# Unused tiles of 64, 192 and 160 bytes ahead of three operand pools in a one-core transformer block

## The chip, the core and the metric

One core of a Trainium2 chip runs the whole kernel. The time is device microseconds from launch to end; the value is the median of several executions. One further execution is taken by the hardware profiler and gives the page and the trace. TensorE (PE in the profile) multiplies: it loads a 128x128 *stationary* operand from SBUF (the row PEld, an LDWEIGHTS instruction) and then streams a *moving* operand of up to 512 columns through it (the row PE, a MATMUL instruction); the product goes to PSUM. VectorE (DVE), ScalarE (ACT) and GpSimd (POOL) do the elementwise work, SyncE (SP) issues the DMAs.

## The reference

One layer of a diffusion backbone on 1024 latent tokens of 1024 channels, with 256 context tokens, in float32. Cut to what is computed:

```python
h  = modulate(rmsnorm(x, g_pre1), sh1, sc1)          # shifts, scales, gates: silu(c) @ w_mod
q, k, v, f, g_a, g_f = split_proj(h @ w_in)          # 1024 x 3328
attn = banded_window_attention(rope(q), rope(k), v, kc, vc, sink)
y  = (sigmoid(g_a) * (attn @ w_pa) + sigmoid(g_f) * (fourier_mix(f) @ w_pf)) @ w_out
x  = x + gt1 * rmsnorm(y, g_post1)
h2 = modulate(rmsnorm(x, g_pre2), sh2, sc2)
u, gate = split(h2 @ w_up)                           # 1024 x 5632
x  = x + gt2 * rmsnorm((silu(conv3(u)) * gate) @ w_down, g_post2)
```

## The kernel before

**Arithmetic.** Every float32 product is made of three passes: each operand is split into a rounded part `hi` (ScalarE) and the remainder `lo` (VectorE or GpSimd), and `mm3` (L83 to L87) issues hi·hi on L85, hi·lo on L86 and lo·hi on L87, each a MATMUL of 512 columns with a fresh 128x128 stationary operand. The three large products (with `w_in`, `w_up`, `w_down`) go by Winograd's form of Strassen's scheme: `wino` (L208) takes *pairs* of weight blocks, and for each pair seven products P1 to P7, so an *item* is one product of one pair, 3 MATMULs for each of its k-blocks (4 in `w_in` and `w_up`, 2 or 3 in `w_down`). Between products, ScalarE and VectorE take results out of PSUM and prepare the next stationary operands.

**Where the operands lie.** The stationary operands (names `hP`, `lP`, `bP`) are 2048-byte tiles of the pool `spool` (`s`, L60). The moving operands are sums of activations or, in the down projection, of `w_down` blocks, with names B11, B21, T1, T2, T3, T4n, B22 (`dB`, `dT` in the down projection). They lie in tiles of 6144 and 2048 bytes that `hb_tiles` (L164) takes from three pools:

- `hb1` (L448, right side of SBUF): all seven moving operands of the product with `w_in`. In the first 80 us some of its tiles also receive `w_mod` blocks.
- `hbl` (L1519, left side, after the small tiles of `small`): B11 and B21 of the product with `w_up`, that is P1 and P2; half of `w_out` (`w0a`, `w0b`); and in the down projection the slots 0 and 1, and half of slot 7, of the rotation in `d_place` (L1734).
- `hb2` (L1928, right side, allocated when the pool `ow` is released): the other five moving operands of `w_up` and the other slots of the down projection.

Pools on the left grow upward in the order of their allocation, pools on the right downward from the top. In the built program every tile of `spool` starts 224 bytes past a multiple of 256, and every tile of `hb1` and `hb2` as well; the tiles of `hbl` start 192 bytes past one. So moving minus stationary address, modulo 256, is 0 for `hb1` and `hb2` and 224 (32 bytes short) for `hbl`. In the attention, the moving operands `kst` and `kc` start at 224 and the stationary queries `qs` (pool `miscA`, left side) at 0.

**Order.** The stages follow each other: norm and modulation with the first items of `w_in` (to about 80 us), the rest of `w_in` (to 335), attention and Fourier mixing (to 530), `w_pa` and `w_out` (to about 690), `w_up` (to about 1120), `w_down` (to the end). Most of it is in blocks of `tc.manual_schedule()`, so engines run in the order of the code. Each engine runs its own queue in order. At the change's place between `ow.release()` (L1927) and `mm(0)` (L1938) the first `w_up` products begin.

Of the kernel before, what the change touches and what calls it, by code (L numbers as in the profile page):

```python
# [10 lines left out]
F = mybir.dt.float32  # L11
# [5 lines left out]
P = 128  # L17
# [18 lines left out]
def fbits(ap):  # L36
    return ap.bitcast(F)
# [3 lines left out]
def block_kernel(ctx: ExitStack, tc: tile.TileContext, t: dict, out: bass.AP, dbg: dict):  # L41
    nc = tc.nc
    PSUM = bass.MemoryType.PSUM

    def pool(name, bufs=1, side=None, space=None):
        kw = {}
        if side:
            kw["side"] = side
        if space:
            kw["space"] = space  # L50
        return tc.alloc_tile_pool(name=name, bufs=bufs, reuse_waits="tile", **kw) if space != bass.MemoryType.DRAM else tc.alloc_tile_pool(name=name, bufs=bufs, space=space)
# [8 lines left out]
    def s(name, dtype=F):  # L60
        return spool.tile([P, 512], dtype, tag="s", name=name, bufs=40)
# [14 lines left out]
    def mul(out, a, b, eng=None):  # L76
        return tt(out, a, b, ALU.mult, eng)

    def split(hi, lo, src, lo_eng=None):
        copy(hi, src)  # L80
        sub(lo, src, fbits(hi), lo_eng)
# [27 lines left out]


    small = pool("small", 1, side="left")

    def tiny(name, n, bufs=4, dtype=F):
        return small.tile([P, n], dtype, tag=f"ty{n}", name=name, bufs=bufs)
# [49 lines left out]
    def hb_tiles(hp, ops, n, ta="ha", tb="hb"):  # L164

        res = {}
        for o in ops:
            a = [hp.tile([P, 3, 512], R, tag=ta, name=f"{o}a{i}", bufs=n) for i in range(2)]
            b = [hp.tile([P, 1, 512], R, tag=tb, name=f"{o}b{i}", bufs=n) for i in range(2)]
            res[o] = list(zip(a, b))  # L170
        return res
# [262 lines left out]
    def ps(name):  # L434
        return psA.tile([P, 512], F, tag="ps", name=name, bufs=8)
# [9 lines left out]
    nc.scalar.activation(out=small.tile([P, 1], F, name="warm"), in_=sv[:, 0:1], func=AF.Sqrt, scale=0.0)  # L445
    mul(sv, sv, vec[:, VC:VC + 16])

    hbp = pool("hb1", 1, side="right")  # L448
    hb = hb_tiles(hbp, ("B11", "T1"), 4, "ga", "gb")

# [417 lines left out]
    def late_loads(i):  # L868
        if i == 0:
            c128.append(s("c128"))  # L870
            load(out=c128[0][:, :2 * P], in_=t["dftc"])
            alt.append(s("alt"))
            load(out=alt[0], in_=t["alt"].to_broadcast([P, 512]))
        elif i == 1:
            for j in range(4):
                wkv[j] = s(f"wkv{j}")
                load(out=wkv[j].rearrange("p (k c) -> p k c", k=2),
                     in_=w_in[j * 256:(j + 1) * 256, K0:K0 + 256].rearrange("(k p) c -> p k c", p=P))
        elif i == 2:
            for j in range(4):  # L880
                wr = wkv[j]
                wkv[j] = (s(f"wkvh{j}", R), s(f"wkvl{j}", R))
                split(*wkv[j], wr)
        elif i == 3:
            for h in range(2):
                vT.append(s(f"vT{h}"))
                load(out=vT[h], in_=v_d[:, h * 512:(h + 1) * 512])
        else:
            for j in range(2):
                dtr[0, j] = s(f"dt0{j}")  # L890
                load(out=dtr[0, j], in_=t["dft"][0, j * P:(j + 1) * P, :])
# [213 lines left out]
    with tc.manual_schedule():  # L1105
        lead(NI - 5)
        lead(NI - 4)
        mm(NI - 5)
        evac(NI - 5)
        for i in range(3, 5):  # L1110
            late_loads(i)
        mm(NI - 4)
        after(NI - 4)
        mm(NI - 3)
        evac(NI - 3)
        c128, alt = c128[0], alt[0]
        ptu = ps("ptu")
        nc.tensor.matmul(ptu[:, :8], c128[:, :P], tu[:, :8], start=True, stop=True)
        nc.tensor.matmul(ptu[:, 8:12], c128[:, P:2 * P], tu[:, 8:12], start=True, stop=True)
        mm(NI - 2)  # L1120
        mm(NI - 1)
        misc.release()
        hbp.release()


        mid = pool("mid", 1, side="right")
        miscA = pool("miscA", 1, side="left")

        def m2(name, dtype=F):
            return mid.tile([P, 512], dtype, tag="m", name=name, bufs=28)  # L1130

        def mp(name, w, dtype=F):
            return mid.tile([P, 640], dtype, tag="p", name=name, bufs=12)[:, :w]

        def m4(name, dtype=F):
            return mid.tile([P, 1024], dtype, tag="l", name=name, bufs=6)

        dtab = {}

        def dft_table(w):  # L1140
            for j in range(2):
                if w == 0:
                    hi, lo = m2(f"dth{w}{j}", R), m2(f"dtl{w}{j}", R)
                else:
                    hi, lo = mp(f"dth{w}{j}", 512, R), mp(f"dtl{w}{j}", 512, R)
                split(hi, lo, dtr[w, j])
                dtab[w, j] = (hi, lo)

        kst = []
        for kv in range(NKV):  # L1150
            kt_ = m4(f"kst{kv}", R)
            load(out=fbits(kt_[0:64, :]), in_=kh_d[kv * 64:(kv + 1) * 64, :])
            load(out=fbits(kt_[64:128, :]), in_=kl_d[kv * 64:(kv + 1) * 64, :])
            kst.append(kt_)
        mask = miscA.tile([P, 1152], F, tag="mask", name="mask")
        load(out=mask, in_=t["mask"])
        snk = miscA.tile([P, NH], F, tag="snk", name="snk")
        load(out=snk, in_=t["sink"].to_broadcast([P, NH]))
        dft_table(0)
        tuo = small.tile([P, 12], F, tag="tuo", name="tuo")  # L1160
        nc.vector.tensor_copy(tuo, ptu[:, :12])
        kc = m2("kc", R)
        for kv in range(NKV):
            load(out=fbits(kc[0:64, kv * L:(kv + 1) * L]), in_=fbits(kcs[0][kv * 64:(kv + 1) * 64, :L]))
            load(out=fbits(kc[64:128, kv * L:(kv + 1) * L]), in_=fbits(kcs[0][kv * 64:(kv + 1) * 64, L:]))
        for j in range(2):
            dtr[1, j] = s(f"dt1{j}")
            load(out=dtr[1, j], in_=t["dft"][1, j * P:(j + 1) * P, :])
        nsnk = miscA.tile([P, NH], F, tag="nsnk", name="nsnk")
        nc.vector.tensor_scalar_mul(nsnk, snk, -1.0)  # L1170
        after(NI - 2)
        evac(NI - 2)
        after(NI - 1)
        evac(NI - 1)
        for k in range(NI, NI + 3):
            after(k)
        psA.release()
# [430 lines left out]
    def x_sq(tk, h):  # L1608
        nc.scalar.activation(out=zn[tk, h], in_=xr[tk][h], func=AF.Square, accum_out=ssy[:, tk + 1, 2 + h:3 + h])
# [278 lines left out]
    with tc.manual_schedule():  # L1888
        for tk in range(NT):
# [35 lines left out]
            x_sq(tk, 0)  # L1925
            x_sq(tk, 1)
        ow.release()  # L1927
        hbp = pool("hb2", 1, side="right")  # L1928
        hb.update(hb_tiles(hbp, OPS[2:], 10))
        mov.update(moving(hb))  # L1930
# [116 lines left out]
    miscD[0].release()  # L2047
    hbl.release()
    hbp.release()
    psC.release()  # L2050
    small.release()
    spool.release()
# [71 lines left out]
```

## Time and profile before

| | |
|---|---|
| median of 3 executions | 1371.83 us (1370.67 to 1372.59) |
| the profiled execution, its own time | 1373.79 us |
| its span, first to last instruction | 1371.9 us |
| mean granted TensorE clock | 0.983 |
| PE busy | 1287.8 us (94%), 5976 MATMULs |
| PEld busy | 1029.8 us (75%), 5976 LDWEIGHTS |
| DVE busy | 1026.1 us (75%) |
| ACT busy | 689.6 us (50%) |
| POOL busy | 500.0 us (36%) |
| DMA, mean | 160 GB/s |

How to read it: successive MATMULs overlap, so the duration of one (about 390 ns for 512 columns) is longer than its place in the stream. What a MATMUL costs is the time from its start to the start of the next, here called the *pitch*. A busy PE is therefore no sign that PE works at its best rate.

### The profile page before, as it was taken

The page shows a single profiled execution, that of the slowest core. Times are in us where ns is not written, and L with a number is a line of the kernel's source. Part 1 is how long each engine was busy: PE and PEld are TensorE (multiplying, and loading weights), DVE is VectorE, ACT ScalarE, POOL GpSimd, SP SyncE. Part 2 cuts the span into 40 slices and gives each one's busy share as a digit, 9 for nine tenths or more (in the row PEclk, how much of TensorE's full clock was granted, in tenths as well). Part 3 has the DMA queues.
Part 4 walks back from the last instruction along what each step waited for, and adds up shares of the span by engine and source line. Part 5 has one row for each costly group of instructions (what it writes and reads, how often), then busy time and mean ns, then how long its engine had stood idle before and what let it go on. Part 6 is the DMA issues. An engine that isn't in the chain of part 4 may idle for free.

```text
span 1371.9 us, 18464 instructions
## 1 busy us (share of the span) xinstructions
PE 1287.8 (94%) x5976; PEld 1029.8 (75%) x5976; DVE 1026.1 (75%) x1729; ACT 689.6 (50%) x1418; POOL 500.0 (36%) x377
## 2 busy tenths in 40 slices
PE   5899999999999999999879999999999988989895
PEld 3558777887878787778667788888888876868674
DVE  4687677874889985735998986666666687796977
ACT  5685336534577773424756554544444454443452
POOL 0000221200333443602593644445444355372754
PEclk9899999999999999999999999999999999999999
DMA  9986284605144346614502554444344569846563
GB/s 306 360 281 192 96 261 135 193 27 161 49 120 127 101 135 200 234 42 128 160 24 85 167 158 128 136 125 132 108 118 113 161 176 295 287 139 227 176 213 123
DMA packets 251124, 219.42 MB, mean 160 GB/s; under 512 B 14972, under 2 KB 204052, under 8 KB 251028
## 3 DMA queue, kind: packets, MB, share of 16 engines
q1 hardware_dynamic: 251028, 218.25, 51.4%
q8 instruction: 47, 0.77, 0.2%
q14 instruction: 49, 0.40, 0.1%
HBM read 159.20 MB, written 58.72 MB: 159 GB/s over the span
## 4 chain that ended last, share of the span: by engine, by line
PE 64%; DVE 19%; issue 5%; ACT 4%; DMA 4%; POOL 3%; SPq 0%; DVEq 0%; POOLq 0%; ACTq 0%
PE X_u L86 5%; PE X_u L87 5%; PE X_u L85 5%; PE Y_u L85 2%; PE Y_u L86 2%; PE Y_u L87 2%; PE X_g L85 2%; PE X_g L87 2%; PE X_g L86 2%; DVE p L1282 2%; DVE pl L68 2%; PE X_d L85 2%; PE X_d L86 2%; PE X_d L87 2%; DVE dT L68 1%
## 5 line engine op out<-in xcount | busy, mean ns | idle before, releaser
L68 DVE TENSOR_TENSOR lP_u<-A_u,hP_u 128x512 fp32r<-128x512 f32 x132 | 102.6, 786 | 45.5 <-ACT hP_u L300 45.5
L362 ACT COPY snP_u<-X_u 128x512 f32<-128x512 f32 x57 | 33.4, 587 | 142.5 <-PE X_u L87 134.0
L68 POOL TENSOR_TENSOR A_u<-A_u,A_u 128x512 f32<-128x512 f32 x44 | 71.4, 1625 | 36.5 <-DVE lP_u L68 18.2
L1302 POOL TENSOR_SCALAR p<-p,sm 128x640 f32<-128x640 f32 (+1 forms) x64 | 48.3, 774 | 84.4 <-PE pp L1307 39.2
L68 POOL TENSOR_TENSOR yd<-yd,snP_d 128x512 f32<-128x512 f32 x36 | 52.1, 1449 | 73.0 <-ACT snP_d L362 73.0
L300 ACT CAST hP_u<-A_u 128x512 fp32r<-128x512 f32 x121 | 74.6, 619 | 0.1
L362 ACT COPY snP_d<-X_d 128x512 f32<-128x512 f32 x48 | 28.0, 584 | 82.5 <-PE X_d L87 82.5
L68 POOL TENSOR_TENSOR A_u<-S_u,A_u 128x512 f32<-128x512 f32 x22 | 29.6, 1343 | 108.8 <-DVE lP_u L68 108.5
L80 ACT CAST ph<-pp 128x512 fp32r<-128x512 f32 x76 | 44.3, 584 | 23.0 <-PE pp L1307 21.7
L68 DVE TENSOR_TENSOR pl<-pp,ph 128x512 fp32r<-128x512 f32 x76 | 51.6, 680 | 3.2 <-ACT ph L80 2.7
L68 POOL TENSOR_TENSOR shk<-shk,rope 128x512 f32<-128x512 f32 x2 | 3.2, 1616 | 135.0 <-DMA A_g<-in_w_in 129.2
L1296 ACT ACTIVATE p<-p,nm 128x640 f32<-128x640 f32 (+1 forms) x64 | 51.4, 802 | 0.7 <-DVE nm L1289 0.7
L68 DVE TENSOR_TENSOR lP_d<-rP_d,hP_d 128x384 fp32r<-128x384 f32 x48 | 43.4, 905 | 10.8 <-ACT hP_d L300 10.5
L1307 PE MATMUL pp<-ident,p 128*128 128x128 f32 x304 | 47.0, 274 | 3.2 <-POOL p L1302 1.8
L1282 DVE CUSTOM_DVE_ANT_0 p<-ss,mask 128x640 f32<-128x640 f32 (+1 forms) x64 | 49.9, 780 | 0.0
L1307 PEld LDWEIGHTS pp<-ident,p 128*128 128x128 f32 x304 | 37.1, 140 | 12.6 <-POOL p L1302 3.7
L68 DVE TENSOR_TENSOR u<-Y_u,snP_u 128x512 f32<-128x512 f32 x22 | 15.2, 691 | 40.3 <-PE Y_u L87 40.3
L1687 DVE SCALAR_TENSOR_TENSOR tb<-u,vec,tb 128x1024 f32<-128x1024 f32 x22 | 39.7, 1805 | 7.3 <-ACT tb L1684 7.2
L68 POOL TENSOR_TENSOR wd<-wd,wd 128x512 f32<-128x512 f32 x22 | 37.0, 1700 | 21.4 <-DVE dB L68 11.5
L68 DVE TENSOR_TENSOR dB<-wd,dB 128x512 fp32r<-128x512 f32 x33 | 38.3, 1170 | 8.5 <-ACT dB L1758 8.4
L68 POOL TENSOR_TENSOR fl<-fr,fh 128x512 fp32r<-128x512 f32 x6 | 7.6, 1287 | 100.0 <-ACT fh L80 99.0
L1612 POOL TENSOR_SCALAR z<-xr,ry 128x512 f32<-128x512 f32 x15 | 16.7, 1123 | 74.5 <-DVE ry L68 64.3
(894 smaller groups left out, 4645.3 us busy)
## 6 DMA issues: line engine op xcount, KB each, us to landing
A_u<-in_w_up SPq DMA_DIRECT2D x88, 256.0 KB, 3.6
wd<-in_w_down SPq DMA_DIRECT2D x55, 256.0 KB, 4.3
wa<-in_w_mod SPq DMA_DIRECT2D x36, 256.0 KB, 5.4
A_g<-in_w_in SPq DMA_DIRECT2D x32, 256.0 KB, 4.9
ws<-in_w_mod SPq DMA_DIRECT2D x30, 256.0 KB, 6.0
wm<-in_w_mod SPq DMA_DIRECT2D x30, 256.0 KB, 4.1
bP_d<-g_d0P SPq DMA_DIRECT2D x56, 128.0 KB, 3.2
x<-in_x SPq DMA_DIRECT2D x16, 256.0 KB, 6.0
```

Source lines behind the costliest of these rows:

```text
L68: return (eng or nc.vector).tensor_tensor(out=out, in0=a, in1=b, op=op)
L80: copy(hi, src)
L85: nc.tensor.matmul(ps, ah, bh, start=start, stop=False, skip_group_check=True)
L86: nc.tensor.matmul(ps, ah, bl, start=False, stop=False, skip_group_check=True)
L87: nc.tensor.matmul(ps, al, bh, start=False, stop=stop, skip_group_check=True)
L300: copy(st[j]["half", p][0], st[j][STA[p]])
L362: copy(d["s" + p], d["X"])
L1282: nc.vector.tensor_tensor_reduce(out=p_, in0=ssc[:, lo:768], in1=self.mk, op0=ALU.add, op1=ALU.max, scale=1.0, scalar=-3.0e38, accum_out=s ...
L1296: nc.scalar.activation(out=self.pt[g], in_=self.pt[g], func=AF.Exp, scale=SCALE, bias=self.m[:, g:g + 1], accum_out=self.sm[:, g:g + 1])
L1302: nc.gpsimd.tensor_scalar(out=self.pt[g], in0=self.pt[g], scalar1=self.sm[:, g:g + 1], scalar2=1.0, op0=ALU.mult, op1=ALU.mult)
L1307: nc.tensor.transpose(pp[:, g * P:(g + 1) * P], self.pt[g][:, j * P:(j + 1) * P], ident)
L1687: nc.vector.scalar_tensor_tensor(out=tb, in0=u[:, 0:1024], scalar=cw[0], in1=tb, op0=ALU.mult, op1=ALU.add)
```

## The change

Three tiles that nothing reads are allocated, each filled with zeros by one GpSimd instruction because a tile must be written once:

- `pad_s`, 64 bytes, as the first tile of `small` on the left. Everything on the left that is allocated after it moves up by 64 bytes: the small tiles, `hbl`, and the pools `miscW`, `miscA`, `miscO`, `miscF`, `miscD`. `const` and `spool` stay.
- `pad_hb1`, 192 bytes, in a pool of its own on the right ahead of `hb1`, released after it.
- `pad_hb2`, 160 bytes, in the same way ahead of `hb2`.

```diff
     small = pool("small", 1, side="left")
+    nc.gpsimd.memset(small.tile([P, 16], F, name="pad_s"), 0.0)
...
+    pad_h = pool("pad_hb1", 1, side="right")
+    nc.gpsimd.memset(pad_h.tile([P, 48], F, name="pad_hb1"), 0.0)
     hbp = pool("hb1", 1, side="right")
...
         hbp.release()
+        pad_h.release()
...
         ow.release()
+        pad_h = pool("pad_hb2", 1, side="right")
+        nc.gpsimd.memset(pad_h.tile([P, 40], F, name="pad_hb2"), 0.0)
         hbp = pool("hb2", 1, side="right")
...
     hbp.release()
+    pad_h.release()
```

In the built program the tiles start, modulo 256 bytes, at:

| | stationary | moving before | moving after | moving minus stationary, before | after |
|---|---|---|---|---|---|
| `hbl` | 224 | 192 | 0 | -32 | +32 |
| `hb1` | 224 | 224 | 32 | 0 | +64 |
| `hb2` | 224 | 224 | 64 | 0 | +96 |
| attention scores (`kst`, `kc` on `qs`) | 0, after 64 | 224 | 224 | -32 | -96 |

No instruction of PE, DVE, ACT or SP is added, and none changes its place. GpSimd gets three instructions. Its queue where the third goes in, in the kernel before (z is the normed residual of a token tile, h the activations of which T1 is a difference; the names in brackets are the semaphores that an instruction waits for):

```order
147 L68 TENSOR_TENSOR B21a_6526<-h_6925,B21a_6525 128x3x128 [waits Activation_49]
148 L68 TENSOR_TENSOR B21b_6528<-h_6925,B21b_6527 128x128 [waits Activation_49]
149 L1612 TENSOR_SCALAR z_7044<-xr_6882,ry_7113 128x512 [waits DVE_49,PE_49,Activation_49]
150 L1612 TENSOR_SCALAR z_7047<-xr_6883,ry_7113 128x512 [waits PE_49,Activation_49]
151 L68 TENSOR_TENSOR h_6671<-h_7015,h_6671 128x512 [waits DMAHW1_49]
```

The same place in the changed kernel:

```order
149 L68 TENSOR_TENSOR B21a_6534<-h_6933,B21a_6533 128x3x128 [waits Activation_49]
150 L68 TENSOR_TENSOR B21b_6536<-h_6933,B21b_6535 128x128 [waits Activation_49]
151 L1618 TENSOR_SCALAR z_7052<-xr_6890,ry_7121 128x512 [waits DVE_49,PE_49,Activation_49]
152 L1618 TENSOR_SCALAR z_7055<-xr_6891,ry_7121 128x512 [waits PE_49,Activation_49]
153 L1935 MEMSET pad_hb_7143 128x40 [waits PE_49]
154 L68 TENSOR_TENSOR h_6679<-h_7023,h_6679 128x512 [waits DMAHW1_49]
```

The memset of `pad_hb2` stands between the two normed halves of a token tile and the first difference for T1, and it waits for PE, because its 160 bytes were part of a tile of `ow` (the value it waits for is that of the first hi·lo MATMUL, L86, in the product of the last token tile with `w_out`).

The shift also lays `kst`, the stacked keys of the attention, over other tiles of `hb1`. Its loads on SP's queue before:

```order
257 L1152 DMA kst_3279<-kh_d 64x1024 [waits DMAHW0_49]
258 L1153 DMA kst_3279<-kl_d 64x1024 [waits DMAHW1_49]
259 L1152 DMA kst_3282<-kh_d 64x1024 [waits DMAHW2_49]
260 L1153 DMA kst_3282<-kl_d 64x1024 [waits DMAHW3_49]
261 L1156 DMA mask<-in_mask 128x1152 [waits DMAHW4_49]
```

And in the changed kernel:

```order
257 L1158 DMA kst_3287<-kh_d 64x1024 [waits DMAHW0_49,PE_49]
258 L1159 DMA kst_3287<-kl_d 64x1024 [waits DMAHW1_49]
259 L1158 DMA kst_3290<-kh_d 64x1024 [waits DMAHW2_49,PE_49]
260 L1159 DMA kst_3290<-kl_d 64x1024 [waits DMAHW3_49]
261 L1162 DMA mask<-in_mask 128x1152 [waits DMAHW4_49]
```

Two of them now wait for PE: for hi·lo MATMULs of the last product with T1 (`Y_g`, L86), which read the `hb1` tile whose last 192 bytes `kst` now covers.

## The prediction

> **What bounds the kernel now.** I read the page's first part and its slices, then busy times by stage, then the timeline of PE inside one stage. The page gives each engine's share, and in 40 slices of 34.3 us the busy tenths of PE and DVE and the granted clock:
>
> ```profile
> span 1371.9 us, 18464 instructions
> PE 1287.8 (94%) x5976; PEld 1029.8 (75%) x5976; DVE 1026.1 (75%) x1729; ACT 689.6 (50%) x1418; POOL 500.0 (36%) x377
> ...
> PE   5899999999999999999879999999999988989895
> ...
> DVE  4687677874889985735998986666666687796977
> ...
> PEclk9899999999999999999999999999999999999999
> ```
>
> PE is nearly always busy, and the clock is granted almost throughout, so the throttle is not the limit. Busy times by stage (us, then PE, PEld, DVE, ACT, POOL with their counts, clock, DMA):
>
> ```profile
> 80.00:335.00 255.00, 253.93 (x1183) 198.25 (x1177) 191.64 (x373) 124.36 (x244) 32.03 (x20) 1.00 0.50 155
> 335.00:530.00 195.00, 185.94 (x1114) 157.29 (x1113) 162.14 (x368) 128.94 (x280) 73.25 (x84) 1.00 0.37 112
> 530.00:700.00 170.00, 158.67 (x695) 125.80 (x694) 112.68 (x202) 76.28 (x194) 67.34 (x56) 0.98 0.45 146
> 700.00:820.00 120.00, 111.86 (x471) 90.12 (x471) 109.83 (x136) 64.22 (x122) 64.72 (x39) 0.97 0.43 121
> 820.00:1120.00 300.00, 298.83 (x1306) 244.83 (x1304) 204.48 (x244) 140.86 (x232) 138.58 (x94) 1.00 0.46 130
> 1120.00:1345.00 225.00, 207.06 (x870) 165.76 (x870) 179.47 (x222) 96.42 (x194) 111.67 (x75) 0.98 0.69 222
> ```
>
> From 80 to 335 us (`w_in`) and from 820 to 1120 us (most of `w_up`) PE has 1.1 and 1.2 us without work: whatever a MATMUL costs there is time of the kernel. From 700 to 820 DVE is busy 109.83 of 120 us beside PE's 111.86, and in the down projection PE is idle 18 of 225 us: there only part of a change in PE's rate would arrive.
>
> So the question is what one MATMUL costs. The timeline of PE in the middle of `w_up` (start us, duration us):
>
> ```profile
> 879.68 0.39 PE L85 MATMUL X_u<-T3a,hP_u 128*128 128x512 f32 x1
> ...
> 882.18 0.39 PE L87 MATMUL X_u<-T3b,lP_u 128*128 128x512 f32 x1
> 882.40 0.40 PE L85 MATMUL X_u<-B11a,hP_u 128*128 128x512 f32 x1
> ...
> 888.01 0.39 PE L85 MATMUL X_u<-T4na,hP_u 128*128 128x512 f32 x1
> ```
>
> The 12 MATMULs of T3 (an `hb2` operand, distance 0) start over 882.40 - 879.68 = 2.72 us: a pitch of 226.7 ns. The 24 of B11 and B21 (`hbl`, distance -32) need 888.01 - 882.40 = 5.61 us: 233.8 ns, with a first one that still belongs to the change of operand; I take 233.4. Nothing differs between them but where the moving operand lies: same shape, same stationary pool, no wait. So an address costs 6.7 ns of a MATMUL here, and this is the quantity that the change moves.
>
> [...]
>
> **The change part by part.**
>
> *The three memsets.* The nearest row is a memset on POOL; beside it the place where the one of `pad_hb2` goes in, and the MATMUL that it waits for:
>
> ```profile
> 666.39 0.39 PE L86 MATMUL y<-wol,mh 128*128 128x512 f32 x1
> ...
> 678.10 2.25 POOL L1612 TENSOR_SCALAR z<-xr,ry 128x512 f32<-128x512 f32 x2 [3.63 <-DVE ry L68]
> 680.32 2.99 POOL L68 TENSOR_TENSOR h<-h,h 128x512 f32<-128x512 f32 x2
> 685.87 0.88 POOL L1612 TENSOR_SCALAR z<-xr,ry 128x512 f32<-128x512 f32 x1 [2.55 <-ACT h L1624]
> 691.75 0.09 POOL L1976 MEMSET u<- 128x1 f32 x1
> ```
>
> The first two memsets run before the first data arrive. The third comes after z at 680.35 us, 14 us after its MATMUL is done, so it waits for nothing; behind it on POOL stand the two differences h (2.99 us), and POOL then idles 2.55 us. 0.1 us, hidden in that gap. Were the cover gone it would cost 0.1 us.
>
> *The loads of `kst`.* They now wait for MATMULs of T1 on L86:
>
> ```profile
> 328.74 0.39 PE L86 MATMUL Y_g<-T1a,hP_g 128*128 128x512 f32 x1
> ...
> 329.42 0.39 PE L86 MATMUL Y_g<-T1b,hP_g 128*128 128x512 f32 x1
> ...
> 328.87 0.48 SPq L1152 DMA_DIRECT2D kst<-kh_d  x1
> 329.41 0.60 SPq L1153 DMA_DIRECT2D kst<-kl_d  x1
> 330.05 0.59 SPq L1152 DMA_DIRECT2D kst<-kh_d  x1
> ...
> L1278 PE MATMUL ss<-kst,qs x128: 278/338/443, 341.8 to 506.6; 128*128 128x384 f32 x96, 128*128 128x256 f32 x32
> ```
>
> The first load is held from 328.87 to 329.13 us, and with it SP's queue of further `kst`, mask, sink and `kc` loads; the second is free by 329.81. The scores first read `kst` at 341.8 us, some 11 us after the last load is issued. A delay of 0.3 us, covered there; nothing.
>
> *The moving operands.* How many MATMULs: `w_in` has 13 pairs x 7 products x 12 = 1092, all on `hb1`. `w_up` has 22 pairs: 22 x 2 x 12 = 528 on `hbl`, 22 x 5 x 12 = 1320 on `hb2`. Half of `w_out` reads `hbl`: 8 token tiles x 8 x 3 = 192. The down projection has 11 k-blocks x 4 x 7 x 3 = 924, of which the rotation puts 300 on `hbl` and 624 on `hb2`. In all 1020 on `hbl`, 1092 on `hb1`, 1944 on `hb2`.
>
> What their pitch will be at +32, +64 and +96 no row of 512 columns shows. Bounds: below, the columns themselves. These rows (min/median/max ns of one) differ in width or address:
>
> ```profile
> L85 PE MATMUL X_u<-B11a,hP_u x66: 394/396/476, 673.9 to 1095.3; 128*128 128x512 f32 x66
> L85 PE MATMUL X_u<-T3a,hP_u x66: 388/389/628, 720.3 to 1111.8; 128*128 128x512 f32 x66
> L85 PE MATMUL ppq<-dth,abh x32: 274/283/365, 343.6 to 367.4; 128*128 128x256 f32 x32
> L1280 PE MATMUL ss<-kc,qs x128: 278/281/288, 342.1 to 506.8; 128*128 128x256 f32 x128
> ```
>
> 256 columns more cost 389 - 283 = 106 ns at distance 0, so 512 columns cost 212 ns and 14.7 ns of the 226.7 are something else: at best, that is gone. [...] Above, 233.4 ns, the worst steady pitch that the trace has. Going from -32 to 0 took off one step of 6.7 ns. I take one more step for all three pools, to 220.0 ns: between the bounds, in the direction in which the only two 512-column rows point, and no lower, since a second step is not shown. That is 13.4 ns for `hbl` and 6.7 ns for `hb1` and `hb2`.
>
> The sum, with the part that arrives:
>
> - `w_in`: 1092 x 6.7 = 7.3 us; all but the first 80 us are bound by PE: 7.0.
> - `w_out`: 192 x 13.4 = 2.6; PE busy 158.67 of 170: 2.3.
> - `w_up`: 1320 x 6.7 + 528 x 13.4 = 8.8 + 7.1 = 15.9. Of its 1848 MATMULs 1306, or 71%, lie from 820 to 1120 us, where all arrives: 11.3; of the other 4.6, beside a busy DVE, half: 2.3.
> - `w_down`: 624 x 6.7 + 300 x 13.4 = 4.2 + 4.0 = 8.2; PE waits here for what DVE and DMA bring, so half: 4.1.
>
> 34.0 us less of PE, 27.0 us less of the kernel: 1373.79 - 27.0 = 1346.8 us for the profiled execution. That one stood 1.96 us over the median of its three, so the median to expect is 1344.8, say 1345 us. With two steps for `hb1` and `hb2` as well, 4056 x 13.4 = 54.4 us of PE, the same eight tenths would be 43 us: 1329; the columns alone, (1020 x 21.4 + 3036 x 14.7) = 66.5 us, would give 1319.
>
> The attention's scores go from -32 to -96: 256 MATMULs, by at most a step each 1.7 us either way, in a stage where DVE works 162 of 195 us; left at 0.
>
> **The rivals.**
>
> *Only `hbl` had a fault.* 226.7 ns is the ordinary cost, some 14 ns of turning from one stationary operand to the next, and -32 adds a collision. For it: the 256-column rows show the same fixed part whatever their address (283 ns at distance 0, 281 at -32). Against it: nothing that I can see in this trace. Then 1020 x 6.7 = 6.8 us of PE, some 5.5 of the kernel: 1366 us.
>
> *Distance 0 was the good place.* The kc row is the warning: it lies 32 bytes short of its queries as `hbl` does, and is not dearer (281 against 283). So distance alone does not set the cost; the moving operand's own place may (192 against 224), and then 0, 32 and 64 are three untried places. If a pitch of 233.4 is what an arbitrary place costs, `hb1` and `hb2` lose what they had: 3036 x 6.7 = 20.3 us of PE, of which 18 arrive, since more PE time is seldom hidden; `hbl` stays: 1390 us. It decides as soon as T1 to B22 in `w_in` and `w_up` show a pitch over 226.7; with `hbl` better by a step meanwhile, 1383.
>
> [...]
>
> **How the numbers follow.** The further step 0.48, only `hbl` 0.20, nothing 0.09, the good place lost 0.23. The predicted time is that of the first, 1345 us; its own range, from two steps everywhere to two thirds of one, is 1324 to 1354. For 8 in 10 the range has to take in 1366 and 1372 and the milder half of the slower case: 1324 to 1383. A measurement of this kernel can tell some 0.2%, 2.7 us, from no change. Faster by more: 0.48 and most of 0.20, 0.65; slower 0.23; the rest, 0.12, within.
>
> **What would show it right or wrong.** In the timeline of PE in the middle of `w_up`, 24 MATMULs of B11 and B21 should start within 5.28 us instead of 5.61, and the 12 of T3 within 2.64 instead of 2.72; the median duration of T3 should fall from 389 to 382 and that of B11 from 396 to 382, while products that the pads do not touch (`pf` in the attention) keep theirs. PE should keep about 99% from 820 us on in a shorter stage; DVE's share rises to 70%. In the down projection PE's idle time should grow. The memset of `pad_hb2` should take 0.1 us without a wait. I am wrong if T3 keeps 389 ns (then only `hbl`), if it rises to 396 (then the good place is lost), or if pitches fall as forecast and the time does not, which would mean that DVE or the DMAs set the stages.

## The result, and the profile after

The changed kernel takes 1380.91 us (median of 4, 1379.14 to 1384.03) against 1371.27 us (median of 4) for the kernel before in the same comparison: a ratio of 1.0073 [1.0058, 1.0088], so it is slower by over 0.2%, where 1345 us was forecast. Its profiled execution took 1384.03 us, 10.2 us more than that of before (1373.79). A ratio here and below is the one on record for its comparison, and can lie up to 0.0006 from the quotient of the two medians. One execution of the kernel before, in the comparison with the last kernel below, took 3383.56 us and is left out of that ratio.

The page after, first lines and PE's slices:

```profile
span 1382.1 us, 18467 instructions
...
PE 1302.5 (94%) x5976; PEld 1028.8 (74%) x5976; DVE 1028.8 (74%) x1729; ACT 689.7 (50%) x1418; POOL 493.6 (36%) x380
...
PE   5899999999999999999879999999999998989896
...
PEclk9999999999999999999989999999999999999998
```

The count of PE's instructions is the same, and PE is busy 14.7 us longer (1302.5 against 1287.8). The clock is granted as before (mean 0.986, before 0.983). So each MATMUL has become dearer. The busy times of the three stages with the long products say where it arrives:

```profile
80.00:335.00 255.00, 253.09 (x1164) 196.31 (x1162) 189.59 (x369) 121.63 (x239) 32.14 (x20) 1.00 0.49 154
...
820.00:1120.00 300.00, 300.00 (x1288) 241.34 (x1287) 201.22 (x239) 137.99 (x226) 127.84 (x93) 1.00 0.45 126
1120.00:1345.00 225.00, 207.22 (x857) 163.02 (x856) 178.63 (x212) 96.45 (x191) 111.18 (x73) 0.98 0.69 218
```

Read the counts, not the shares: in the same 300 us from 820 us on, PE starts 1288 MATMULs where it started 1306, with no idle time left at all. The share of busy time hardly moved (298.83 to 300.00); the work done in it fell by 1.4% by the records.

The timeline of PE in the middle of `w_up`, at the same product as in the prediction (start us, duration us):

```profile
882.42 0.39 PE L85 MATMUL X_u<-T3a,hP_u 128*128 128x512 f32 x1
...
885.22 0.39 PE L85 MATMUL X_u<-B11a,hP_u 128*128 128x512 f32 x1
...
890.82 0.39 PE L85 MATMUL X_u<-T4na,hP_u 128*128 128x512 f32 x1
```

The 12 MATMULs of T3 (`hb2`, now +96) take 885.22 - 882.42 = 2.80 us, 233.3 ns each, against 226.7 before. The 24 of B11 and B21 (`hbl`, now +32) take 890.82 - 885.22 = 5.60 us, 233.3 ns each: what they took at -32. `hb2` lost the good rate, and `hbl` did not gain it. The same by groups (min/median/max ns of one), with the operand of `hb1` below:

```profile
L85 PE MATMUL X_u<-B11a,hP_u x66: 391/394/476, 674.1 to 1102.1; 128*128 128x512 f32 x66
L85 PE MATMUL X_u<-T3a,hP_u x66: 392/394/628, 720.8 to 1118.9; 128*128 128x512 f32 x66
L86 PE MATMUL X_u<-T3a,hP_u x66: 392/399/628, 721.8 to 1119.2; 128*128 128x512 f32 x66
L85 PE MATMUL Y_g<-T1a,hP_g x24: 388/394/502, 70.9 to 330.4; 128*128 128x512 f32 x24
```

T3 had a median of 389 ns before; it has 394 and 399 now. From the starts of all back-to-back MATMULs of 512 columns, the mean pitch in `w_in` went from 227.7 to 230.6 ns (`hb1`, +64), in `w_up` from 227.2 to 233.3 (`hb2`) and from 233.4 to 233.2 (`hbl`). The price on PE is 1944 x 6.0 = 11.7 us for `hb2` and 1092 x 2.9 = 3.2 us for `hb1`, 14.9 us together, close to the 14.7 us of the page.

Where it arrived, by the start of the last MATMUL of each stage: end of `w_in` 338.8 to 340.8 us (+2.0), of `w_out` 673.6 to 673.9 (+0.3: the attention and the small products between gave 1.7 us back in this execution), of `w_up` 1126.5 to 1133.1 (+6.6), of `w_down` 1361.5 to 1371.6 (+10.1). Each of these comes from one execution a kernel, and they scatter: from the end of `w_in` to that of `w_out`, where the pads change little, the nine kept traces of the layer take 332.8 to 336.3 us.

The edits that were costed at nothing did cost nothing. POOL's timeline around the third memset:

```profile
678.33 2.24 POOL L1618 TENSOR_SCALAR z<-xr,ry 128x512 f32<-128x512 f32 x2 [3.63 <-DVE ry L68]
680.52 0.13 POOL L1935 MEMSET pad_hb<- 128x40 f32 x1
680.61 2.98 POOL L68 TENSOR_TENSOR h<-h,h 128x512 f32<-128x512 f32 x2
```

SP's queue at the first loads of `kst`:

```profile
331.07 0.48 SPq L1158 DMA_DIRECT2D kst<-kh_d  x1
331.61 0.59 SPq L1159 DMA_DIRECT2D kst<-kl_d  x1
```

And the scores that read them, min/median/max ns and first to last start:

```profile
L1284 PE MATMUL ss<-kst,qs x128: 279/341/448, 343.8 to 508.6; 128*128 128x384 f32 x96, 128*128 128x256 f32 x32
```

The memset takes 0.13 us and waits for nothing; the `kst` loads start 2.2 us later than before (331.07 against 328.87), nearly all of it because `w_in` ends 2.0 us later; the rest fits the new wait (the last L86 on T1a starts at 330.64, takes 0.40 and ends at 331.04), and the scores still begin 12.7 us after the first of them (12.9 before).

### The profile page after: what moved, and what is told of

It is laid out like the page before. It is cut to its first block, busy times and chain, and to the rows that moved or that the text cites. A ratio compares the mean times of both kernels' runs of the same rounds, so it can differ in the third digit from the quotient of the medians.

```text
span 1382.1 us, 18467 instructions
## 1 busy us (share of the span) xinstructions
PE 1302.5 (94%) x5976; PEld 1028.8 (74%) x5976; DVE 1028.8 (74%) x1729; ACT 689.7 (50%) x1418; POOL 493.6 (36%) x380
## 4 chain that ended last, share of the span: by engine, by line
PE 63%; DVE 17%; DMA 7%; issue 5%; ACT 3%; POOL 2%; SPq 1%; DVEq 0%; POOLq 0%; ACTq 0%
PE X_u L86 5%; PE X_u L87 5%; PE X_u L85 5%; PE Y_u L85 3%; PE Y_u L86 3%; PE Y_u L87 3%; PE X_g L85 2%; PE X_g L86 2%; PE X_g L87 2%; DMA wa<-in_w_mod 2%; DVE p L1288 2%; DMA ws<-in_w_mod 2%; DVE pl L68 2%; PE X_d L85 2%; PE X_d L86 2%
## 5 line engine op out<-in xcount | busy, mean ns | idle before, releaser
L68 DVE TENSOR_TENSOR lP_u<-A_u,hP_u 128x512 fp32r<-128x512 f32 x132 | 108.9, 834 | 49.4 <-ACT hP_u L303 49.4
L68 POOL TENSOR_TENSOR A_u<-A_u,A_u 128x512 f32<-128x512 f32 x44 | 67.9, 1545 | 39.2 <-DVE lP_u L68 18.9
L68 DVE TENSOR_TENSOR lP_d<-rP_d,hP_d 128x384 fp32r<-128x384 f32 x48 | 42.3, 882 | 10.9 <-ACT hP_d L303 10.9
L1693 DVE SCALAR_TENSOR_TENSOR tb<-u,vec,tb 128x1024 f32<-128x1024 f32 x22 | 43.9, 1996 | 4.7 <-ACT tb L1690 4.6
L68 POOL TENSOR_TENSOR wd<-wd,wd 128x512 f32<-128x512 f32 x22 | 37.4, 1716 | 22.0 <-DVE dB L68 11.7
L68 POOL TENSOR_TENSOR fl<-fr,fh 128x512 fp32r<-128x512 f32 x6 | 7.6, 1288 | 101.7 <-ACT fh L80 101.2
```

What stands on the lines that cost most here:

```text
L68: return (eng or nc.vector).tensor_tensor(out=out, in0=a, in1=b, op=op)
L1693: nc.vector.scalar_tensor_tensor(out=tb, in0=u[:, 0:1024], scalar=cw[0], in1=tb, op0=ALU.mult, op1=ALU.add)
```

## Experiments

All layer kernels below are the kernel before with pads of other sizes. "Distance" is the moving minus the stationary address modulo 256.

**The map.** A small kernel of its own holds one moving and one stationary tile and runs groups of 20 or 32 back-to-back MATMULs, each group at another distance. Nothing of the layer is computed (the output is a copy of `x`), so only the pitches count, not its time. The core of it:

```python
def run(name, am, as_, w=512, n=N):
    p = ps.tile([P, 512], F, tag="ps", name=name, bufs=4)
    for i in range(n):
        a, s = am // 4, as_ // 4 + i % 4 * P
        nc.tensor.matmul(p[:, :w], st[:, s:s + P], mv[:, a:a + w], start=True, stop=True, skip_group_check=True)
...
run("d" + x, 32 * k, 0)          # moving operand moved
run("both" + x, 32 * k, 32 * k)  # both moved
run("s" + x, 0, 32 * k)          # stationary operand moved
run("fine" + chr(97 + k // 8) + chr(97 + k % 8), 4 * k, 0)
run("h" + x, 32 * k, 0, 256, 32)
```

> A kernel of its own that computes nothing of the layer (its output is a copy of x): runs of 20 or 32 MATMULs without a wait, each with its own 128x128 stationary operand, float32 rounded as in the layer, at chosen start addresses modulo 256 bytes. Groups d: moving at 0, 32, ... 224, stationary at 0. Groups both: both at 0, 32, ... 224. Groups s: moving at 0, stationary at 0, 32, ... 224. Groups fine: moving at 0, 4, ... 252, stationary at 0. Groups h and q: as d, with 256 and 384 columns. Theory 1 (the distance of moving from stationary sets the pitch, and 0 is a good place): all both-groups near 226.7 ns; d at 0 226.7, at 32 and 96 about 233, at 64 about 231, at 224 233; s the mirror of d (stationary 32 later is like moving 32 earlier). Theory 2 (the moving operand's own address sets the pitch): both varies as d does, and all s-groups are equal. Theory 3 (neither: what differs is other traffic of the layer's stages): all groups of 512 columns equal.

Groups of the map, the last two numbers before the idle time being busy us and mean ns of one:

```profile
L35 PE MATMUL finehf<-mv,st 128*128 128x512 f32 x20 | 5.0, 403 | 0.0
...
L35 PE MATMUL donesixty<-mv,st 128*128 128x512 f32 x20 | 4.8, 396 | 0.0
...
L35 PE MATMUL dninetysix<-mv,st 128*128 128x512 f32 x20 | 4.8, 396 | 0.0
...
L35 PE MATMUL dthirtytwo<-mv,st 128*128 128x512 f32 x20 | 4.8, 395 | 0.0
...
L35 PE MATMUL dtwotwofour<-mv,st 128*128 128x512 f32 x20 | 4.8, 395 | 0.0
...
L35 PE MATMUL dsixtyfour<-mv,st 128*128 128x512 f32 x20 | 4.7, 392 | 0.0
...
L35 PE MATMUL bothsixtyfour<-mv,st 128*128 128x512 f32 x20 | 4.7, 391 | 0.0
...
L35 PE MATMUL dzero<-mv,st 128*128 128x512 f32 x20 | 4.7, 389 | 0.0
...
L35 PE MATMUL hzero<-mv,st 128*128 128x256 f32 x32 | 4.0, 283 | 0.0
...
L35 PE MATMUL honeninetytwo<-mv,st 128*128 128x256 f32 x32 | 3.8, 277 | 0.0
```

In a steady stream the duration lies some 160 to 163 ns over the pitch (389 at 226.7), so the durations already rank the distances roughly. The steady pitches, from the starts after a group's first eight MATMULs (good to some 0.4 ns, by which of the rest are taken):

| moving minus stationary | 0 | 32 | 64 | 96 | 128 | 160 | 192 | 224 |
|---|---|---|---|---|---|---|---|---|
| 512 columns, ns | 226.7 | 233.3 | 228.8 | 233.3 | 233.3 | 234.0 | 233.3 | 233.3 |
| 256 columns, ns | 120.0 | 117.8 | 117.8 | 120.0 | 118.8 | 117.3 | 113.3 | 118.3 |

With both operands moved by the same amount every group settles at 226.7 (the mean of 391 at "bothsixtyfour" contains its first, unsettled MATMULs); with the stationary operand moved instead, the values mirror those above to within 0.7 ns (192 gives 228.8, the value of 64). In steps of 4 bytes, no distance goes under 226.7: 0, 28, 60, 108, 156 and 252 reach it, and 100, 120, 132, 196 and 244 ("finehf") cost up to 240.0. So for 512 columns the distance sets the pitch, the place of the moving operand alone does not, and 0 is a minimum, not a point on a slope. The other theories of the expectation fall. Five of these distances (0, 32, 64, 96 and 224) were measured again in the second small kernel below, and came out the same to 0.1 ns.

**All three distances 0.** 32 bytes ahead of `small` and no other pad; this is the counter-test, which gives `hbl` what `hb1` and `hb2` had.

```diff
     small = pool("small", 1, side="left")
+    nc.gpsimd.memset(small.tile([P, 8], F, name="pad_s"), 0.0)
```

> The kernel before with one pad of 32 bytes ahead of the small tiles and no other: hbl, hb1 and hb2 all lie at distance 0 (all operands 224 past a multiple of 256). Theories 1 and 2: B11 and B21 in w_up fall from 233.4 to 226.7 ns like T3, 1020 x 6.7 = 6.8 us of PE, some 5.5 us of the kernel: 1366 us, ratio to before 0.996. Theory 3: 1371 us.

1363.42 us (5 runs) against 1370.25 (15): 0.9948 [0.9936, 0.9961], faster than both kernels. Its groups:

```profile
L85 PE MATMUL X_u<-B11a,hP_u x66: 387/389/477, 671.2 to 1087.9; 128*128 128x512 f32 x66
...
L85 PE MATMUL X_u<-T3a,hP_u x66: 388/389/393, 718.3 to 1104.2; 128*128 128x512 f32 x66
```

B11 falls from 396 to T3's 389 ns; the mean pitch is 226.8 in `w_up`, for both pools. By the medians 6.8 us came, the best of this study, where 5.5 were expected from 1020 x 6.7 = 6.8 us of PE. PE gained more than that sum: the operands of `hb2`, which lay at 0 before too, no longer follow a change of distance (see below) and fall from 227.2 to 226.8 in `w_up`, and the mean of all of `w_down` falls from 229.8 to 227.0. Together with `w_out` that is some 7.9 us of PE.

**The distances kept, the places moved.** 96 bytes ahead of `spool` and 160 ahead of `hb1` and `hb2`: every operand of the three large products lies elsewhere, and every distance in them is that of before. (In the built program 288 MATMULs of `w_out` and of the Fourier mixing change theirs; at the prices of the map that makes some 0.6 us less of PE.)

```diff
+    nc.gpsimd.memset(spool.tile([P, 24], F, name="pad_c"), 0.0)
...
+    nc.gpsimd.memset(pad_h.tile([P, 40], F, name="pad_hb1"), 0.0)
...
+        nc.gpsimd.memset(pad_h.tile([P, 40], F, name="pad_hb2"), 0.0)
```

> All stationary tiles are moved by 96 bytes (to 64 modulo 256), hb1 and hb2 by 96 as well (to 64), hbl by 96 (to 32): every distance is that of the kernel before (0, 0, -32) at other addresses. Theory 1: T3 226.7 ns, B11 233.4, time as before, 1371 us (ratio 1.000). Theory 2: T3 no longer at 224, so about 233 ns and 1380 us or more.

1370.90 us (10 runs), 1.0004 [0.9994, 1.0015]: no change. The groups (one line further down in this kernel) are those of before, 396 for B11 and 389 for T3:

```profile
L86 PE MATMUL X_u<-B11a,hP_u x66: 395/396/479, 673.7 to 1093.6; 128*128 128x512 f32 x66
...
L86 PE MATMUL X_u<-T3a,hP_u x66: 388/389/397, 720.9 to 1110.1; 128*128 128x512 f32 x66
```

With it the theory of the place falls in the layer as well.

**Three other distances.** Pads of 160, 96 and 64 bytes: `hbl` at 128, `hb1` at 160, `hb2` at 192.

```diff
+    nc.gpsimd.memset(small.tile([P, 40], F, name="pad_s"), 0.0)
...
+    nc.gpsimd.memset(pad_h.tile([P, 24], F, name="pad_hb1"), 0.0)
...
+        nc.gpsimd.memset(pad_h.tile([P, 16], F, name="pad_hb2"), 0.0)
```

> As the changed kernel with pads of 160, 96 and 64 bytes: hbl at distance 128, hb1 at 160, hb2 at 192. Theory 1 with 0 as the only good place: pitches of 231 to 236 ns in all three, about 1380 to 1384 us. If a good window lies on this side: below 226.7 ns in one of them.

1384.82 us (4 runs), 1.0108 [1.0094, 1.0122]. The pitches are 234.2 ns for `hb1` in `w_in` (the map has 234.0), 233.2 for `hb2` (233.3) and 232.3 for `hbl` (233.3) in `w_up`:

```profile
L85 PE MATMUL X_u<-T3a,hP_u x66: 393/394/398, 724.3 to 1119.3; 128*128 128x512 f32 x66
```

Here the map foretells the layer to 1 ns a MATMUL. It is the slowest of all, since `hb1`, which the changed kernel puts at the milder distance 64, now pays 6.5 ns too.

**One pad at a time.** The three parts of the change, each alone.

```diff
+    nc.gpsimd.memset(small.tile([P, 16], F, name="pad_s"), 0.0)
```

> The 64 bytes ahead of the small tiles alone: hbl from -32 to +32, hb1 and hb2 at 0. By the map, +32 costs what -32 costs (233.3 ns), so the time is that of the kernel before, 1370 us, ratio 1.000. If the shift of the other pools on the left costs something by itself, it shows here.

```diff
+    nc.gpsimd.memset(pad_h.tile([P, 48], F, name="pad_hb1"), 0.0)
```

> The 192 bytes ahead of hb1 alone: w_in at +64, 230.6 ns against 227.7 in the layer: 1092 x 2.9 = 3.2 us of PE, 2 to 3 us of the kernel, ratio 1.002.

```diff
+        nc.gpsimd.memset(pad_h.tile([P, 40], F, name="pad_hb2"), 0.0)
```

> The 160 bytes ahead of hb2 alone: 1944 MATMULs at +96, 233.4 against 227.4 ns: 11.7 us of PE, 7 to 8 us of the kernel, ratio 1.0055; with the part of hb1 it should make up the 1.0073 of the whole change.

| pad | time | ratio | pitch that it moves |
|---|---|---|---|
| `hbl` to +32 | 1371.41 us (12 runs) | 1.0000 [0.9991, 1.0009] | 233.4 to 233.5 |
| `hb1` to +64 | 1373.83 us (11 runs) | 1.0018 [1.0010, 1.0027] | 227.7 to 230.6 |
| `hb2` to +96 | 1380.78 us (5 runs) | 1.0067 [1.0055, 1.0079] | 227.2 to 233.4 |

The whole change is `hb2` and a little `hb1`. The three excesses add up to 0.0085, the change measured 0.0073 [0.0058, 0.0088]: within the intervals. `hb2` alone cost more than I had expected of it, 0.0067 against 0.0055, though 0.0055 is still the edge of its interval; its MATMULs of `w_up` and `w_down` cost 1944 x 6.2 = 12 us of PE, of which 0.0067 x 1370.7 = 9.2 us arrived (10.0 us by the medians).

**One pool at the middling distance.** As with all distances 0, but `hb2` at +64, which the map gives 228.8 ns.

```diff
+    nc.gpsimd.memset(small.tile([P, 8], F, name="pad_s"), 0.0)
...
+        nc.gpsimd.memset(pad_h.tile([P, 48], F, name="pad_hb2"), 0.0)
```

> The kernel with every distance at 0 (1363.4 us, ratio 0.9948), but with 192 bytes ahead of hb2, so that hb2 alone lies at +64. A test of whether the map foretells a time: 228.8 to 228.9 ns in steady runs against 226.7, in the layer perhaps 229.5 with the starts of the runs; 1944 MATMULs x 2.5 = 4.9 us of PE, of which the share that arrived when hb2 went to +96 (9.2 us of the 11.7 worked out) makes 3.8 us: 1367 us, ratio 0.9975. If the time comes out at 0.9948 or at 1.001 (as at +96), the map does not carry over.

1369.74 us (11 runs) against 1372.19 (15), 0.9986 [0.9976, 0.9996]: dearer than expected. The groups in `w_up`:

```profile
L85 PE MATMUL X_u<-B11a,hP_u x66: 387/397/477, 670.0 to 1090.3; 128*128 128x512 f32 x66
L86 PE MATMUL X_u<-B11a,hP_u x66: 387/389/499, 671.1 to 1090.6; 128*128 128x512 f32 x66
...
L85 PE MATMUL X_u<-T3a,hP_u x66: 392/394/398, 717.9 to 1106.8; 128*128 128x512 f32 x66
```

From 820 to 1090 us the products in the middle of a run have the map's pitches, 228.9 ns for T3 (+64) and 226.7 for B21 (0). But the first product after a change of distance is dearer: B11, which follows T3, costs 230.8 ns in the mean though it lies at 0, and T4n, which follows B21, 230.3. A stream needs some MATMULs to settle, and a kernel whose pools lie at different distances can pay for that: here 12 x (230.8 - 226.7) + 12 x (230.3 - 228.9) = 66 ns for a pair, 1.5 us for the 22 pairs of `w_up`.

The run missed its expected ratio of 0.9975 by 0.0011, which is 1.5 us; 0.9975 lies just outside the interval. That the two figures of 1.5 us are equal is chance, since the part of T4n was in the 229.5 ns expected for `hb2`, and not all of PE's time arrives. The sum over all of it, against the kernel with all distances 0: in `w_up` `hb2` rose from 226.8 to 229.3 ns, as expected (1320 x 2.5 = 3.3 us), but `hbl`, still at 0, rose too, from 226.9 to 228.7 (528 x 1.8 = 1.0 us); in `w_down` the mean rose from 227.0 to 230.8 (924 x 3.8 = 3.5 us, where 624 x 2.5 = 1.6 were expected). That is 7.8 us of PE instead of 4.9, and 0.9986 - 0.9948 = 0.0038, or 5.2 us, of time, 67% of it. So the expectation had the share that arrives about right and left out what the neighbours of the moved pool pay. This is argued from the pitches; no run took the changes of distance away and kept the +64.

**Is it the load of the stationary operand?** The map again with fewer stationary columns, with the same stationary tile every time, and with bfloat16 operands. Nothing of the layer is computed here either.

```diff
-    def run(name, am, as_, w=512, n=N):
+    def run(name, am, as_, w=512, n=N, m=P, same=False):
...
+            a, s = am // 4, as_ // 4 + (0 if same else i % 4 * P)
+            nc.tensor.matmul(p[:m, :w], st[:, s:s + m], mv[:, a:a + w], start=True, stop=True, skip_group_check=True)
...
+            nc.tensor.matmul(p, sb16[:, s:s + P], mb16[:, a:a + 512], start=True, stop=True, skip_group_check=True)
```

> Again a kernel that computes nothing of the layer (its output is a copy of x): runs of 20 MATMULs of 512 columns, moving at 0, 32, 64, 96 and 224, stationary at 0. Groups full, three, half, quarter: stationary operands of 128, 96, 64 and 32 columns. Group same: the same stationary address every time instead of four in turn. Groups b: both operands in bfloat16, at 0, 32, ... 224. Theory 1a (the 13.3 ns over the 213.3 of the columns are collisions of the two reads while the stationary operand is loaded): the pitch falls with fewer stationary columns, about 220 ns at half and 216 to 217 at a quarter, and the spread over distances shrinks with it; bfloat16, which reads half the bytes, lies lower too. Theory 1b (226.7 ns is a fixed turn-round, and only the 6.7 ns above it are collisions): 226.7 ns stays at distance 0 whatever the stationary columns and the type, and only the spread shrinks.

The 213.3 ns of the columns can be worked out from the first map, as an estimate: 256 columns more cost 226.7 - 120.0 = 106.7 ns there at distance 0, and 512 columns twice that.

```profile
L40 PE MATMUL quartertwotwofour<-mv,st 128*32 128x512 f32 x20 | 4.9, 399 | 0.0
...
L40 PE MATMUL fullthirtytwo<-mv,st 128*128 128x512 f32 x20 | 4.8, 395 | 0.0
...
L40 PE MATMUL quarterzero<-mv,st 128*32 128x512 f32 x20 | 4.8, 394 | 0.0
...
L40 PE MATMUL fullzero<-mv,st 128*128 128x512 f32 x20 | 4.7, 389 | 0.0
L40 PE MATMUL samezero<-mv,st 128*128 128x512 f32 x20 | 4.7, 389 | 0.0
L46 PE MATMUL bthirtytwo<-mb,sb 128*128 128x512 bf16 x20 | 4.5, 379 | 0.0
...
L46 PE MATMUL bonetwoeight<-mb,sb 128*128 128x512 bf16 x20 | 4.5, 379 | 0.0
```

The loads of the stationary operands in the same run:

```profile
L46 PEld LDWEIGHTS <-sb 128*128 128x128 bf16 x160 | 15.6, 98 | 18.9 <-issue 0.3
...
L40 PEld LDWEIGHTS fullzero<-mv,st 128*128 128x128 f32 x20 | 3.8, 188 | 0.8
...
L40 PEld LDWEIGHTS quarterzero<-mv,st 128*32 128x32 f32 x20 | 2.2, 109 | 2.4
```

Fewer stationary columns make a shorter load (109 ns for 32 columns, 188 for 128), but the pitch does not fall with it: at distance 0 it is 226.7 ns with 128 columns, 230 with 96, 230.5 with 64, 231.7 with 32. At the other four distances it moves by -4.5 to +6.6 ns, without order, and no group comes under 226.7. The guess that the price shrinks with the load falls. With the same stationary tile every time the pitches are those of four tiles in turn. In bfloat16 every one of the eight distances has 215.8 ns, 10.9 ns less than the float32 groups at their best (four groups lack one of their 20 records, and the gap there is left out), so the guess of a fixed time for turning to the next stationary operand, the same for all types, falls too. What remains shown is that the price belongs to the float32 operands (226.7 to 234.0 ns over the eight distances of the first map) and not to the bfloat16 ones (215.8 at all eight), and depends on where the two lie relative to each other. What makes the difference between the types is not separated: both operands were narrowed at once, and the load became shorter with them (98 ns). The shorter load alone is not it, since 109 ns for 32 float32 columns left the pitch at 231.7. By what mechanism the distance sets the pitch was not shown.

## Why the prediction was wrong, point by point

- **What bounds the kernel.** Right. In the stage from 820 us, PE was busy 298.83 of 300 us and is now 300.00, and a dearer MATMUL there came out as time: `w_up` took 6.3 us longer, of 1320 x 6.1 = 8.1 us on PE, 78%.
- **The quantity.** Right in kind: the distance of the two operands sets the pitch, 6.7 ns between -32 and 0. The runs settled what one row could not: the same distances at other addresses change nothing (1.0004), the operand of `hbl` alone brought to 0 brings 0.9948. That the distance does nothing, given a chance of 0.09 and 1372 us in the range, no run with float32 operands shows: their pitch goes from 226.7 to 240.0 ns over the 64 distances of the map, and the change took 1380.91 us. It is so for the bfloat16 ones (215.8 ns at every distance).
- **The step that failed.** "I take one more step for all three pools, to 220.0 ns." It drew a line through two distances, -32 and 0, and went on along it. Measured at +32, +64 and +96: 233.2, 230.6 and 233.3 ns in the layer, 233.3, 228.8 and 233.3 in the map. The step has the wrong sign for `hb1` (+2.9 for -6.7 ns) and `hb2` (+6.1 for -6.7), and for `hbl` the forecast fall of 13.4 is 0. Both bounds that were set (212 to 233.4) held; the choice between them was the error. At 0 the pitch was already as low as any of 64 distances in steps of 4 bytes makes it, so none of these distances could have brought `hb1` and `hb2` anything; `hbl` had 6.7 ns to gain, at 0. The measured 1380.91 us lies within the range that was stated, but only because the range took in part of the rival that came true.
- **The argument from 256 columns.** The row of `kc`, at -32 and yet not dearer than one at 0, was read as "distance alone does not set the cost". It does not transfer: with 256 columns 0 is among the dearest distances (120.0 ns, against 118.3 at 224 and 113.3 at 192). A row of another width was no witness. The common part of 14.7 ns was worked out nearly right: the map has 120.0, 173.4 and 226.7 ns at distance 0 for 256, 384 and 512 columns, 53.3 ns for each 128 columns and 13.4 beside them. The error was to take it for something that a better address removes. For 256 columns some of it goes (113.3 at 192); for 512 columns none does at any of the 64 distances.
- **The share that arrives.** The sum gave 34.0 us of PE and 27.0 of the kernel, 79%. Measured: 14.7 us of PE, 10.2 us of the profiled execution, 69%. One pad at a time, over many executions, 9.2 of 12 us arrived for `hb2` and 0.0018 x 1370.7 = 2.5 of 3.2 for `hb1`, 77% and 78%. The forecast share was not far off; what was wrong is what it was a share of. By stage single traces do not settle it. In the down projection +3.5 us came for 624 x 5.5 = 3.4, where half was assumed, but with the pad of `hb2` alone the same stage is as long as before (235.1 us both times). PE's two largest groups of waits there, in the changed kernel (total us, times, longest):

```profile
PE Y_d L85 <- DVE yd L68: 8.5, 6, 2.4
...
PE X_d L85 <- ACT snP_d L365: 5.4, 4, 2.3
```

These are ten waits, of 2.4 us at most (before, eleven of 2.6 at most). Whether PE's idle time in the down projection, 18 us before and after, takes up a dearer MATMUL there stays open.
- **The sums.** Two steps everywhere was worked out as 1329 us and stands in the range as 1324. Nothing else hangs on it.
- **The edits at nothing.** Right: the memset 0.13 us without a wait, the `kst` loads and the scores moved with the end of `w_in`. The scores at -96 keep their median for `kc` (280 ns after, 281 before):

```profile
L1286 PE MATMUL ss<-kc,qs x128: 276/280/287, 344.2 to 508.9; 128*128 128x256 f32 x128
```

- **The rivals.** "Distance 0 was the good place" is what happened, by the sign it named: T3 rose to 394 and 399 ns. Its size was 1390 us with 6.7 ns for both pools; `hb1` at +64 lost only 2.9, of the 14.7 us of PE 69% arrived where 18 of 20.3 us were assumed, and 1380.91 came. "Only `hbl` had a fault" came near in its price (5.5 us less; with all distances 0, 6.8 less), but +32 does not mend it, and the fixed time of some 14 ns that it gave every MATMUL is down to some 2.6 ns in bfloat16, by an estimate (215.8, less four times the 53.3 ns that 128 columns take in float32; no bfloat16 run has another width).

## What to carry to other kernels

Where float32 matmuls of 512 columns, split as here, run back to back on a full PE, give the moving and the stationary operands the same address modulo 256; here the 32 bytes that did it for one pool were worth 0.5%, and any other multiple of 32 cost 2 to 8 ns of each MATMUL in the map. Two groups of one shape and different pitch are the sign to look for, and the operands' addresses the first thing to compare. Two measured distances give no direction: a small kernel of its own maps them all in one run, and its map held in the layer to about 2 ns.

## What the runs showed that I had not expected

- In the changed kernel B11 and T3, at different distances (+32 and +96), have the same mean pitch of 233.3 ns. In the map 31 of the 64 distances share one of three values, 226.7, 233.3 or 240.0 ns, rather than rising gradually.
- After a change of distance a stream at a cheap distance needs several MATMULs to settle; the first twelve cost 1.4 to 4.1 ns more each in the kernel with `hb2` at +64. The kernel before paid this too: its T4n, at distance 0 but after B21 at -32, had 228.7 ns where T3 had 226.7. With all distances equal it has 226.7. Between two dear distances the change costs nothing: in the changed kernel T4n, at +96 after B21 at +32, has 233.0 ns. And in the map a group also has to settle when both operands move to another address at the same distance ("bothsixtyfour" starts with pitches of 224 to 236 ns), so it is best to give all operands of alternating products one address modulo 256.
- The best distance depends on the width: 0 for 512 columns (226.7 ns), 192 for 256 columns (113.3 against 120.0 at 0).
